# Written orders for the prologue and for the end of the convolution, tap products on four row groups, and late weight splits queued behind other work

## The chip, the cores and the metric

The kernel runs on one core of one Trainium2 chip. The metric is the device time in microseconds (us) of one execution; lower is better. All inputs and the output are fp32.

## The reference

Two layers of a diffusion backbone over 512 tokens of width 1024, with 256 context tokens. Layer 0 mixes with a long convolution (Hyena, 512 channels) beside a neighbourhood attention, layer 1 with a Conformer convolution module; each is followed by a gated feed-forward part of width 2816. Every part is wrapped in two RMS norms with shift, scale and gate from a conditioning vector. What the change touches:

```python
m = jax.nn.silu(cond) @ w_mod + b_mod              # six vectors of 1024: shift, scale, gate, twice
hn = rms_norm(h, g_mix_pre) * (1 + scale1) + shift1
...
# layer 0: the long filters
hdn = jnp.sin(freq[0] * (z @ w1 + b1))             # z: 512 x 33, hidden width 64
hdn = jnp.sin(freq[1] * (hdn @ w2 + b2))
hdn = jnp.sin(freq[2] * (hdn @ w3 + b3))
filt = hdn @ w4                                    # 512 x 1024: forward and backward filter
return filt[:, :512] * decay, filt[:, 512:] * decay
...
# layer 1: the Conformer module
a, g = jnp.split(t @ w_pw1 + b_pw1, 2, axis=-1)
u = a * jax.nn.sigmoid(g)
u = dwconv(u, w_dw, b_dw)                          # 31 taps a channel
u = jax.nn.silu(layer_norm(u, ln_g, ln_b))
return u @ w_pw2 + b_pw2
```

## The kernel before

The tokens lie on the 128 partitions in four chunks, t = 0 to 3. TensorE (PE) does all products. The big ones are three fp32r products each (`mm3`, L278 to L282): the high part of one operand with both parts of the other and its low part with the high one. So every weight block of 512 KB is loaded raw by SP into one of three `raw` buffers and split: ScalarE (ACT) casts the high part (L297), VectorE (DVE) subtracts it for the low part (L298). The class `Stream` issues loads and splits a few blocks ahead of use. The outputs of a split go to working tiles `w`, or to kept tiles `wk` for blocks that are needed again.

A scheduler places all instructions by its own estimate, except on the engines named in a `tc.manual_schedule` block, on which the order of the program text holds. Before, the prologue has such a block for PE alone, in the order of a string of keys ("1 x0 x1 2 x2 x3 3 t0 ... k11"); ACT, DVE, GpSimd (POOL) and SP are placed by the scheduler.

**Prologue.** A small network makes the filters of the long convolution: three layers (PE products at L686, L693 and L716), each followed by a reduction of turns on DVE (L662 to L664, tile `sx`) and a Sin on ACT (L665, tiles `hdn`, then `h`). The two filters (`filt`, keys a and b) are four products each with `w4x` (L743), multiplied with the decay `dec` (L745), split (L746, L747) and negated (L750). `w4x` is first completed by a product on POOL (L710) and two ACT instructions (L717, L718). Meanwhile the four chunks of x get their norm: the sum of squares on ACT (L408), the root on POOL (L401, L403), the scaling on DVE (L498), and are transposed on PE (L705, key t, `pt`) and copied out (L706). The conditioning product (L674, key g, tile `g` from the landed blocks `land`) has eight steps; step k writes to the group of 32 columns k mod 4. The filter spectra (`kspec`, key k, tile `pk`) are mm3 products of the filters with a cosine table, whose high and low part `TFh`, `TFl` come from `tfr` (L727, L728). `columns` (L792) turns the conditioning product to columns, `modulate` applies it, and then the input projection `pz` begins.

**Conformer.** The first pointwise product (`pg`) runs in two halves of 512 channels; `glu` makes `u`. The convolution over time is done as short Fourier transforms: `taps` (L1373) transforms the 31 taps, four products 31 rows deep, each copied to `H` by ACT (L1374); `c_fwd` transforms `u` to `dr` and `di`; `c_prod` (L1404 to L1412) multiplies with `H`, six DVE instructions but for one addition on POOL (L1406), and splits the result to `Yh` and `Yl`; `c_inv` transforms back (`po`), adds the bias (L1426) and takes statistics (L1427); `ln` (L1431 to L1435) norms `yc`; `to_T` transposes it (L515), applies SiLU (ACT, L1438) and splits it into `hTh` (L521) and `hTl` (L522). `gemm_td` is the second pointwise product (`acc`): first all steps k over chunks 0 and 1 for the blocks that are not kept, then per chunk the kept ones, then chunks 2 and 3, whose transposes (`late`) come between. Here no order is written; the scheduler chose it for all engines.

## Time and profile before

| | us |
|---|---|
| median of 3 runs | 1267.14 |
| lowest, highest run | 1264.29, 1267.49 |
| profiled execution | 1264.98 |
| its span in the trace | 1263.2 |

| engine | busy us | share of the span |
|---|---|---|
| PE (TensorE) | 1239.3 | 98% |
| DVE (VectorE) | 815.2 | 65% |
| ACT (ScalarE) | 509.2 | 40% |
| POOL (GpSimd) | 89.4 | 7% |

In rows of the timeline the first number is the start in us from the start of the span, the second the time up to the end of the last instruction of the row; then engine, line, operation, written tile <- read tiles, shapes and count. In brackets stands the idle time of the engine ahead of it and what ended it. A product's own time includes its way through the array, so that products in a row overlap; their pace is read from the starts. An fp32 product leaves two records, an fp32r product or a transpose one. PEld is the loading of weights into the array.

### The profile page before, as it was taken

The page shows a single profiled execution, that of the slowest core. Times are in us where ns is not written, and L with a number is a line of the kernel's source. Part 1 is how long each engine was busy: PE and PEld are TensorE (multiplying, and loading weights), DVE is VectorE, ACT ScalarE, POOL GpSimd, SP SyncE. Part 2 cuts the span into 40 slices and gives each one's busy share as a digit, 9 for nine tenths or more (in the row PEclk, how much of TensorE's full clock was granted, in tenths as well). Part 3 has the DMA queues.
Part 4 walks back from the last instruction along what each step waited for, and adds up shares of the span by engine and source line. Part 5 has one row for each costly group of instructions (what it writes and reads, how often), then busy time and mean ns, then how long its engine had stood idle before and what let it go on. Part 6 is the DMA issues. An engine that isn't in the chain of part 4 may idle for free.

```text
span 1263.2 us, 15493 instructions
## 1 busy us (share of the span) xinstructions
PE 1239.3 (98%) x6044; PEld 1024.2 (81%) x6044; DVE 815.2 (65%) x1072; ACT 509.2 (40%) x788; POOL 89.4 (7%) x157
## 2 busy tenths in 40 slices
PE   6999999999999999999999999999999999999997
PEld 3688888988898888887888887878988888888886
DVE  4577696876567788778534576686687555566233
ACT  5453333576443332336223442233544333344221
POOL 3110000231200000000000100012100000000001
PEclk9999999999999999999999999999999999999999
DMA  9535434743136577764344331120265233332321
GB/s 351 192 114 170 133 110 142 257 152 128 40 101 216 184 240 245 226 193 146 117 132 135 131 104 55 50 101 1 68 203 178 88 98 100 100 100 90 95 84 66
DMA packets 47865, 171.64 MB, mean 136 GB/s; under 512 B 5741, under 2 KB 5772, under 8 KB 47792
## 3 DMA queue, kind: packets, MB, share of 16 engines
q1 hardware_dynamic: 47428, 169.93, 41.4%
q8 instruction: 47, 0.77, 0.2%
q0 software_dynamic: 176, 0.40, 0.1%
q10 hardware_dynamic: 188, 0.33, 0.1%
q14 instruction: 26, 0.21, 0.1%
HBM read 167.76 MB, written 2.10 MB: 134 GB/s over the span
## 4 chain that ended last, share of the span: by engine, by line
PE 76%; DMA 9%; DVE 9%; ACT 2%; issue 2%; POOL 1%; DVEq 0%; POOLq 0%; ACTq 0%
PE pz L280 11%; PE pz L281 11%; PE pz L282 11%; PE acc L282 8%; PE acc L280 8%; PE acc L281 8%; DMA raw<-in_wup 4%; DMA raw<-in_wcol 4%; DVE w L298 3%; PE pg L280 2%; PE pg L282 2%; PE pg L281 2%; DVE acc L430 2%; DMA raw<-in_wgate 1%; ACT w L297 1%
## 5 line engine op out<-in xcount | busy, mean ns | idle before, releaser
L281 PE MATMUL pz<-hTl,w 128*128 128x512 f32 (+1 forms) x920 | 345.4, 376 | 0.0
L280 PE MATMUL pz<-hTh,w 128*128 128x512 f32 (+1 forms) x920 | 344.6, 377 | 0.5 <-DVE hTh L521 0.5
L282 PE MATMUL pz<-hTh,w 128*128 128x512 f32 (+1 forms) x920 | 345.1, 376 | 0.0
L298 DVE TENSOR_TENSOR w<-raw,w 128x1024 fp32r<-128x1024 f32 x159 | 193.9, 1222 | 199.9 <-ACT w L297 194.0
L297 ACT CAST w<-raw 128x1024 fp32r<-128x1024 f32 x159 | 166.4, 1051 | 331.8 <-PE pz L281 132.0
L282 PEld LDWEIGHTS pz<-hTh,w 128*128 128x128 f32 x920 | 173.8, 189 | 31.4
L281 PEld LDWEIGHTS pz<-hTl,w 128*128 128x128 f32 x920 | 173.8, 189 | 30.0 <-DVE hTl L522 0.4
L280 PEld LDWEIGHTS pz<-hTh,w 128*128 128x128 f32 x920 | 173.0, 189 | 31.0 <-DVE hTh L521 1.0
L430 DVE SCALAR_TENSOR_TENSOR acc<-raw,sc,acc 128x1024 f32<-128x1024 f32 x74 | 95.4, 1289 | 41.4 <-DMA raw<-in_wgate 20.8
L281 PE MATMUL acc<-w,gs 128*128 128x512 f32 x256 | 99.6, 389 | 0.0
L282 PE MATMUL acc<-w,gs 128*128 128x512 f32 x256 | 98.4, 390 | 0.5 <-DVE gs L1317 0.5
L280 PE MATMUL acc<-w,gs 128*128 128x512 f32 x256 | 97.0, 389 | 0.0
L879 ACT ACTIVATE cv<-pz,pk 128x512 f32<-128x512 f32 x88 | 67.6, 772 | 0.7 <-PE pz L282 0.7
L881 DVE SCALAR_TENSOR_TENSOR cv<-pz,pk,cv 128x511 f32<-128x511 f32 x88 | 65.6, 747 | 1.8
L880 DVE SCALAR_TENSOR_TENSOR cv<-pz,pk,cv 128x511 f32<-128x511 f32 x88 | 65.1, 744 | 0.2 <-ACT cv L879 0.2
L1279 ACT ACTIVATE cv<-cv 128x512 f32<-128x512 f32 x44 | 27.7, 629 | 81.6 <-DVE cv L881 81.5
L282 PEld LDWEIGHTS acc<-w,gs 128*128 128x128 f32 x256 | 48.0, 188 | 10.9 <-DVE gs L1317 0.9
L280 PEld LDWEIGHTS acc<-w,gs 128*128 128x128 f32 x256 | 48.1, 188 | 10.1 <-DVE cv L881 0.2
L281 PEld LDWEIGHTS acc<-w,gs 128*128 128x128 f32 x256 | 48.1, 188 | 9.9
L298 DVE TENSOR_TENSOR wk<-raw,wk 128x1024 fp32r<-128x1024 f32 x30 | 37.1, 1245 | 29.0 <-ACT wk L297 28.9
L536 DVE TENSOR_TENSOR py<-acc,gg 128x512 f32<-128x512 f32 x32 | 21.8, 688 | 49.1 <-ACT py L408 49.1
L399 POOL TENSOR_SCALAR t<-t,t 128x1 f32<-128x1 f32 x19 | 7.0, 369 | 636.6 <-ACT py L408 628.1
(327 smaller groups left out, 1934.5 us busy)
## 6 DMA issues: line engine op xcount, KB each, us to landing
raw<-in_wup SPq DMA_DIRECT2D x88, 512.0 KB, 3.6
raw<-in_wcol SPq DMA_DIRECT2D x48, 512.0 KB, 4.6
raw<-in_wdn SPq DMA_DIRECT2D x44, 512.0 KB, 3.6
raw<-in_wgate SPq DMA_DIRECT2D x32, 512.0 KB, 4.4
raw<-in_pw SPq DMA_DIRECT2D x24, 512.0 KB, 3.9
raw<-in_win SPq DMA_DIRECT2D x20, 512.0 KB, 3.5
land<-in_wmod SPq DMA_DIRECT2D x16, 512.0 KB, 10.4
BM<-in_rpb SPq DMA_DIRECT2D x8, 512.0 KB, 3.4
```

Of the source, the lines that this page charges most:

```text
L280: PE.matmul(o, ah, bh, start=start, stop=False)
L281: PE.matmul(o, ah, bl, start=False, stop=False)
L282: PE.matmul(o, al, bh, start=False, stop=stop)
L297: A.copy(hi, r)
L298: V.tensor_tensor(lo, r, f(hi), op=ALU.subtract)
L399: G.tensor_scalar(v, sums[0], sums[1], EPS, op0=ALU.add, op1=ALU.add)
L430: V.scalar_tensor_tensor(acc, rs[k], ck_, init if k == 0 else acc, op0=ALU.mult, op1=ALU.add)
L536: V.tensor_tensor(p_[:, sl], y2[i], gg[:, sl], op=ALU.mult)
L879: A.activation(dst, pz, AF.Identity, bias=pc(bk, i), scale=pc(wk + "1", i))
L880: V.scalar_tensor_tensor(dst[:, 1:w], pz[:, 0:w - 1], pc(wk + "0", i), dst[:, 1:w], op0=ALU.mult, op1=ALU.add)
L881: V.scalar_tensor_tensor(dst[:, 0:w - 1], pz[:, 1:w], pc(wk + "2", i), dst[:, 0:w - 1], op0=ALU.mult, op1=ALU.add)
L1279: A.activation(cv[:, 0], cv[:, 0], AF.Silu, bias=0.0, scale=1.0)
```

## The change

The computation stays the same; the change has five parts.

1. **Prologue.** PE, ACT and DVE follow the program order up to the end of filter b, PE alone from there to the end of the prologue. 23 dummy products of a zero tile `warm` (128 by 128, fp32) are put on PE ahead of layer 1 (5), behind it (3), ahead of layer 3 (5) and ahead of filter a (10). The steps are cut finer: sums of squares (`x_sum`) and scalings (`x_scale`) apart, layer 3 and its reduction apart, filters by channel group and step. The two ACT instructions on `w4x` go behind the first and the second Sin. Filter a follows the third Sin, then four of the eight transposes with the table split, then filter b; the other transposes stand between halves of the spectra. The eight steps of the conditioning product become two batches of four. SP loads the decay ahead of the table.
2. **Taps.** The four tap products get operands padded to 32 rows and laid on four groups of 32 partitions, so that each has rows of its own, and are issued together behind the first half's `glu`, into four PSUM tiles.
3. **c_prod.** The addition goes from POOL to DVE, cast and low part are done in halves.
4. **End of the convolution.** From the first pointwise product of chunk 3 to the end of the second pointwise product PE follows the program: the inverse transforms of chunk 1 before the last step of the first pointwise product, those of the first half's chunks 2 and 3 behind it, then the transposes, the last forward transform, and the steps k = 0 to 2 of the second pointwise product before the inverse transforms that need the last `c_prod`.
5. **Late splits.** While `behind` holds an instruction, the scheduler queues the low-part subtractions of new splits behind it: behind the last one of `to_T`, then behind the last one of `c_prod`, until the last inverse transforms are issued.

On ACT, the start of the prologue up to the third Sin. Before (L717, L718: `w4x`; L665: Sin; L408: sums of squares):

```order
L717 ACTIVATE w4x_80<-w4x_80 64x512
L372 CAST onesr<-ones 128x128
L387 COPY SCT_117<-sc 128x8
L392 ACTIVATE SCT_117<-pk 128x8
L718 COPY w4x_80<-w4x_80 64x512
L665 ACTIVATE hdn_180<-sx_190 128x256
L408 ACTIVATE junk_195,t_196<-xc_84 128x1024
L408 ACTIVATE junk_203,t_204<-xc_85 128x1024
L408 ACTIVATE junk_219,t_220<-xc_86 128x1024
L665 ACTIVATE hdn_180<-sx_214 128x256
L408 ACTIVATE junk_227,t_228<-xc_87 128x1024
L665 ACTIVATE h_59_246<-sx_247 128x512
```

After (the same steps at L735, L741, L686 and L426):

```order
L390 CAST onesr<-ones 128x128
L405 COPY SCT_120<-sc 128x8
L410 ACTIVATE SCT_120<-pk 128x8
L686 ACTIVATE hdn_183<-sx_198 128x256
L735 ACTIVATE w4x_83<-w4x_83 64x512
L426 ACTIVATE xn_208,t_209<-xc_87 128x1024
L686 ACTIVATE hdn_183<-sx_218 128x256
L426 ACTIVATE xn_228,t_229<-xc_88 128x1024
L741 COPY w4x_83<-w4x_83 64x512
L426 ACTIVATE xn_255,t_256<-xc_89 128x1024
L426 ACTIVATE xn_262,t_263<-xc_90 128x1024
L686 ACTIVATE h_59_269<-sx_270 128x512
```

Both `w4x` instructions stood ahead of the first Sin; now one stands behind the first and the other behind the second, and the sums are spread 1, 1 and 2 between the Sins.

On PE, the first place of the conditioning product (L674) before, between the last transposes and the filters (L743, all eight in a row):

```order
L674 MATMUL g_311<-land_146,SCT_117 32x512
L674 MATMUL g_313<-land_146,SCT_117 32x512
L674 MATMUL g_315<-land_148,SCT_117 32x512
L674 MATMUL g_317<-land_148,SCT_117 32x512
L743 MATMUL pf_319<-w4x_80,h_59_246 128x512
L743 MATMUL pf_325<-w4x_80,h_59_246 128x512
L743 MATMUL pf_331<-w4x_80,h_59_246 128x512
L743 MATMUL pf_337<-w4x_80,h_59_246 128x512
L743 MATMUL pf_347<-w4x_80,h_59_246 128x512
L743 MATMUL pf_353<-w4x_80,h_59_246 128x512
L743 MATMUL pf_359<-w4x_80,h_59_246 128x512
L743 MATMUL pf_365<-w4x_80,h_59_246 128x512
```

After, the start of its first batch (L695), behind the fourth half of the spectra and long behind both filters:

```order
L695 MATMUL g_460<-land_149,SCT_120 32x512
L695 MATMUL g_460<-land_153,SCT_120 32x512
L695 MATMUL g_460<-land_157,SCT_120 32x512
L695 MATMUL g_460<-land_161,SCT_120 32x512
L695 MATMUL g_465<-land_149,SCT_120 32x512
L695 MATMUL g_465<-land_153,SCT_120 32x512
L695 MATMUL g_465<-land_157,SCT_120 32x512
L695 MATMUL g_465<-land_161,SCT_120 32x512
L695 MATMUL g_470<-land_151,SCT_120 32x512
L695 MATMUL g_470<-land_155,SCT_120 32x512
L695 MATMUL g_470<-land_159,SCT_120 32x512
L695 MATMUL g_470<-land_163,SCT_120 32x512
```

Step 0 ran alone, and steps 1 to 3 came after the filters; now four steps, one for each group of 32 columns, stand next to one another for each output tile `g`.

On DVE, the second half's middle `c_prod` before (L1404 to L1412), where the tiles `wk` are low parts of weights (L298):

```order
L1404 TENSOR_TENSOR cy_6754<-dr_6740,H_6165 128x512
L1408 TENSOR_TENSOR ct_6755<-dr_6740,H_6166 128x512
L298 TENSOR_TENSOR wk_6964<-raw_6925,wk_6963 128x1024
L1405 TENSOR_TENSOR ct_6755<-di_6741,H_6166 128x512
L1407 TENSOR_TENSOR cy_6754<-di_6741,H_6165 128x512
L298 TENSOR_TENSOR wk_6982<-raw_6927,wk_6981 128x1024
L298 TENSOR_TENSOR wk_7000<-raw_6949,wk_6999 128x1024
L1409 TENSOR_TENSOR cy_6754<-cy_6754,ct_6755 128x512
L298 TENSOR_TENSOR wk_7006<-raw_6967,wk_7005 128x1024
L1412 TENSOR_TENSOR Yl_6763<-cy_6754,Yh_6762 128x1024
L1426 TENSOR_TENSOR yc_6791<-po_6790,bd_6167 128x512
```

After, the last `c_prod` (L1516 to L1521) with the splits (L305) around it:

```order
L1516 TENSOR_TENSOR cy_6948<-dr_6934,H_6194 128x512
L1517 TENSOR_TENSOR ct_6949<-di_6935,H_6195 128x512
L1516 TENSOR_TENSOR cy_6948<-di_6935,H_6194 128x512
L1517 TENSOR_TENSOR ct_6949<-dr_6934,H_6195 128x512
L305 TENSOR_TENSOR w_6965<-raw_6524,w_6964 128x1024
L1518 TENSOR_TENSOR cy_6948<-cy_6948,ct_6949 128x512 x2
L1521 TENSOR_TENSOR Yl_6951<-cy_6948,Yh_6950 128x512 x2
L305 TENSOR_TENSOR w_6989<-raw_6530,w_6988 128x1024
L305 TENSOR_TENSOR wk_7007<-raw_6968,wk_7006 128x1024
L305 TENSOR_TENSOR wk_7061<-raw_6970,wk_7060 128x1024
```

Four subtractions stood inside one `c_prod`, between its steps; in the new order one does inside the last `c_prod`, and the next ones stand behind its `Yl`.

The diff, cut to its core:

```diff
+    k31 = np.concatenate([k31, np.zeros((1, 256))], 0)
+    k31 = np.concatenate([k31[:, :128]] * 2 + [k31[:, 128:]] * 2, 0)
...
+    wd = np.concatenate([g["cf_w_dw"][0], np.zeros_like(g["cf_w_dw"][0][:1])], 0)
+    a["wdw"] = np.concatenate([wd[:, :512], wd[:, 512:]] * 2, 0)
...
-        V.tensor_tensor(lo, r, f(hi), op=ALU.subtract)
+        with ExitStack() as queued:
+            if behind:
+                queued.enter_context(tc.issue_after(behind[0]))
+            V.tensor_tensor(lo, r, f(hi), op=ALU.subtract)
         return hi, lo
...
+    warm = cpool.tile([P, P], F32, name="warm")
+    V.memset(warm, 0.0)
+    warm_ps = pspool.tile([P, 512], F32, name="warm_ps", tag="ps")
+
+    def warm_up(n):
+        for _ in range(n):
+            PE.matmul(warm_ps[:, 0:P], warm, warm, start=True, stop=True)
 
...
-            V.tensor_tensor(hT[1][kp][:, :, sl], X, f(o_h), op=ALU.subtract)
+            done = V.tensor_tensor(hT[1][kp][:, :, sl], X, f(o_h), op=ALU.subtract)
+        return done
...
+            if k in between:
+                between[k]()
...
-    for key in "x0 x1 x2 x3 t0 t1 d0 d1 l0 l1 l2 l3 l4 l5 l6 l7 l8 l9 l10 l11 l12 l13 l14 l15".split():
+    for key in "x0 x1 x2 x3 d0 d1 t0 t1 l0 l1 l2 l3 l4 l5 l6 l7 l8 l9 l10 l11 l12 l13 l14 l15".split():
...
-    def x_norm(c):
-        xns[c] = norm_chunk(xc[c])
+    def x_sum(c):
+        xns[c] = s4(F32, (P, 1024), "xn")
+        xns[c, "r"] = rstd([sumsq(xc[c], xns[c])])
+
+    def x_scale(c):
+        V.tensor_scalar(xns[c], xc[c], xns[c, "r"], None, op0=ALU.mult)
...
+    def w4_neg():
+        A.mul(w4x[0:64, 512:1024], w4x[0:64, 0:512], -1.0)
+
+    def w4_decay():
         G.tensor_tensor(w4x[64:128, 0:512], w4x[64:128, 0:512], zt[64:128, 512:1024], op=ALU.mult)
-        pm = [ps("pf") for _ in range(2)]
...
+    def w4_copy():
         A.copy(w4x[64:128, 512:1024], w4x[64:128, 0:512])
...
-        for i in range(2):
-            hv = flat(TFh[i], "p a b -> p (a b)")
-            with tc.issue_after(sin3.ins):
-                A.copy(hv, tfr[i])
-            V.tensor_tensor(flat(TFl[i], "p a b -> p (a b)"), tfr[i], f(hv), op=ALU.subtract)
...
+    early = ExitStack()
+    early.enter_context(tc.manual_schedule(engines={mybir.EngineType.PE, mybir.EngineType.Activation,
+                                                    mybir.EngineType.DVE}))
+    warm_up(5)
+    layer1()
+    warm_up(3)
+    w4_decay()
+    w4_neg()
+    x_sum(0)
+    layer2()
+    warm_up(5)
+    x_sum(1)
+    x_scale(0)
+    layer3(0)
+    warm_up(10)
+    w4_copy()
+    x_sum(2)
+    x_sum(3)
+    layer3(1)
+    for ch in range(4):
+        filt("a", ch, "p")
+    x_scale(1)
+    x_scale(2)
+    filt("a", 0, "m")
+    filt("a", 1, "m")
+    x_scale(3)
+    filt("a", 0, "l")
+    for ch in (2, 3):
+        filt("a", ch, "m")
+        filt("a", ch - 1, "l")
+    filt("a", 3, "l")
+    for i in range(2):
+        x_T(i)
+        table_hi(i)
+        table_lo(i)
+    for i in range(2, 4):
+        x_T(i)
+    for ch in range(4):
+        filt("b", ch, "p")
+        filt("b", ch, "m")
+        if ch:
+            filt("b", ch - 1, "l")
+    filt("b", 3, "l")
+    early.close()
     order_pe = ExitStack()
     order_pe.enter_context(tc.manual_schedule(engines={mybir.EngineType.PE}))
-    for key in "1 x0 x1 2 x2 x3 3 t0 t1 t2 t3 t4 t5 t6 t7 g0 a b g123 k00 k01 g4567 k100 c m k101 k11".split():
-        steps[key[0]](*(int(i) for i in key[1:]))
+    kspec(0, 0, 0)
+    x_T(4)
+    x_T(5)
+    for lo in range(2):
+        negate("a", lo)
+    kspec(1, 0, 0)
+    x_T(6)
+    x_T(7)
+    for lo in range(2):
+        negate("b", lo)
+    kspec(0, 0, 1)
+    kspec(1, 0, 1)
+    gemv_k(0, 1, 2, 3)
+    gemv_k(4, 5, 6, 7)
+    kspec(0, 1, 0)
+    columns()
+    modulate()
+    kspec(0, 1, 1)
+    kspec(1, 1)
     order_pe.close()
     hT = hTs[0]
 
@@ -1359,19 +1463,23 @@
...
-    SP.dma_start(kk[:31, 0:256], a["k31"])
+    SP.dma_start(kk[:, 0:128], a["k31"])
     wd = s4(F32, (P, 1024), "wd")
-    SP.dma_start(wd[:31], a["wdw"])
+    SP.dma_start(wd[:, 0:512], a["wdw"])
...
-    def taps(cs, hf):
-        pm = ps("pm")
-        PE.matmul(pm, kk[:31, cs * P:(cs + 1) * P], wd[:31, hf * 512:(hf + 1) * 512], start=True, stop=True)
-        A.copy(H[cs][:, hf * 512:(hf + 1) * 512], pm)
+
+    def taps():
+        pms = [ps("pm") for _ in range(4)]
+        for i, pm in enumerate(pms):
+            rs = slice(32 * i, 32 * i + 32)
+            PE.matmul(pm, kk[rs, 0:P], wd[rs, 0:512], start=True, stop=True)
+        for i in (0, 2, 1, 3):
+            A.copy(H[i // 2][:, i % 2 * 512:(i % 2 + 1) * 512], pms[i])
...
-        V.tensor_tensor(y[:, 0], pr_, H[0][:, hs], op=ALU.mult)
-        V.tensor_tensor(tm[:, 0], pi_, H[1][:, hs], op=ALU.mult)
-        G.tensor_tensor(y[:, 0], y[:, 0], tm[:, 0], op=ALU.add)
-        V.tensor_tensor(y[:, 1], pi_, H[0][:, hs], op=ALU.mult)
-        V.tensor_tensor(tm[:, 1], pr_, H[1][:, hs], op=ALU.mult)
-        V.tensor_tensor(y[:, 1], y[:, 1], tm[:, 1], op=ALU.subtract)
         yh_, yl_ = s4(F32R, n="Yh"), s4(F32R, n="Yl")
-        A.copy(yh_, y)
-        V.tensor_tensor(yl_, y, f(yh_), op=ALU.subtract)
+        for i, (p0, p1, op) in enumerate(((pr_, pi_, ALU.add), (pi_, pr_, ALU.subtract))):
+            V.tensor_tensor(y[:, i], p0, H[0][:, hs], op=ALU.mult)
+            V.tensor_tensor(tm[:, i], p1, H[1][:, hs], op=ALU.mult)
+            V.tensor_tensor(y[:, i], y[:, i], tm[:, i], op=op)
+            A.copy(yh_[:, i], y[:, i])
+        for i in range(2):
+            done = V.tensor_tensor(yl_[:, i], y[:, i], f(yh_[:, i]), op=ALU.subtract)
+        prod_end[:] = [done.ins]
         return yh_, yl_
 
     parts = {0: [(0, 0)], 1: [(0, 1), (1, 2)], 2: [(1, 1), (2, 2)], 3: [(2, 3)]}
...
-    taps(0, 0)
+    taps()
...
-        if k < 3:
-            taps(1 - k % 2, (k + 1) // 2)
...
+    last = ExitStack()
+    last.enter_context(tc.manual_schedule(engines={mybir.EngineType.PE}))
     pw1_t(3, range(4), True, False)
     Y1.append(c_prod(1, *c_fwd(1, U1)))
-    pw1_t(3, range(4, 8), False, False)
-    c_inv(0, 2, Y0)
+    pw1_t(3, range(4, 7), False, False)
     c_inv(1, 1, Y1)
     ln(1)
-    U1.append(glu(1, 3))
+    pw1_t(3, range(7, 8), False, True)
     mark("ln+pw2")
-    fw = c_fwd(2, U1)
+    c_inv(0, 2, Y0)
+    c_inv(0, 3, Y0)
     lT = alloc_hT()
-    to_T([yc[0], yc[1]], 0, lT, silu_ev)
-    Y1.append(c_prod(1, *fw))
-    c_inv(0, 3, Y0)
+    behind.append(to_T([yc[0], yc[1]], 0, lT, silu_ev).ins)
+    Y1.append(c_prod(1, *c_fwd(2, U1)))
     dmp("cd", yc[0])
     b2 = s4(F32, (P, 1024), "b2")
     SP.dma_start(b2, a["bpw2"].rearrange("a b -> (a b)").partition_broadcast(P))
...
+    def third():
+        behind[:] = prod_end
+
+    def fourth():
         for t in (2, 3):
             c_inv(1, t, Y1)
+        for t in (2, 3):
             ln(t)
+        behind.clear()
+
+    def late1():
         to_T([yc[2], yc[3]], 1, lT, silu_ev)
 
     after, late2, st2 = stage_end(1, 1, 1, 2, pre=add_b2)
     gemm_td(8, 4, lambda k: (hk(lT, k, 0), hk(lT, k, 1)), after, 4,
-            late=late1)
+            late=late1, between={0: third, 2: fourth})
+    last.close()
     hT = st2["hT"]
     dmp("h3", h[0])
```

More of the change, by code (lines that the diff above doesn't have):

```diff
@@ L541, in post_chunk, with gemm_td @@
             V.scalar_tensor_tensor(hc[:, sl], p_[:, sl], r, hc[:, sl], op0=ALU.mult, op1=ALU.add)
-    def gemm_td(nk, keep, act, after, nxt, late=None, nbg=2):
+    def gemm_td(nk, keep, act, after, nxt, late=None, nbg=2, between={}):
         acc = [[None, None] for _ in range(4)]
@@ new lines, in layer3 @@
+    def layer3(part):
+        if part == 0:
+            pm = [ps("pf") for _ in range(2)]
+            h3s.append(pm)
+            for i, o, src, ro in ((0, slice(0, 256), slice(0, 256), 0), (1, slice(256, 512), slice(0, 256), 0),
+                                  (0, slice(0, 255), slice(1, 256), 64), (0, slice(255, 256), slice(255, 256), 64),
+                                  (1, slice(255, 511), slice(0, 256), 64), (1, slice(511, 512), slice(255, 256), 64)):
+                rs = slice(64 * i, 64 * i + 64)
+                PE.matmul(pm[i][ro:ro + 64, o], fl[rs, 128:192], h2[rs, src], start=True, stop=True)
+            return
+        pm = h3s.pop()
@@ L719, in layer3, with table_hi @@
         h3s.append(s4(F32, (P, 1024), "h3"))
-        sin3 = sin_stage([(pm[0], slice(None), slice(0, 256)), (pm[1], slice(None), slice(256, 512)),
-                          (pm[1], slice(64, 128), slice(255, 256))], 2, h3s[0][:, 0:512], 512)
+        sin_stage([(pm[0], slice(None), slice(0, 256)), (pm[1], slice(None), slice(256, 512)),
+                   (pm[1], slice(64, 128), slice(255, 256))], 2, h3s[0][:, 0:512], 512)
         G.memset(h3s[0][64:128, 511:512], 0.0)
-        for i in range(2):
-            hv = flat(TFh[i], "p a b -> p (a b)")
-            with tc.issue_after(sin3.ins):
-                A.copy(hv, tfr[i])
-            V.tensor_tensor(flat(TFl[i], "p a b -> p (a b)"), tfr[i], f(hv), op=ALU.subtract)
+    def table_hi(i):
+        A.copy(flat(TFh[i], "p a b -> p (a b)"), tfr[i])
@@ L730, in tfs, with table_lo @@
+    def table_lo(i):
+        V.tensor_tensor(flat(TFl[i], "p a b -> p (a b)"), tfr[i], f(flat(TFh[i], "p a b -> p (a b)")), op=ALU.subtract)
     def tfs(lo, ch, cs, fc):
```

40 lines of the change are left out of this document (18 added, 22 removed).

## The prediction, made before the changed kernel was run

> **What bounds the kernel now.** I read the profiled execution from the top: the page's busy line, then the busy time in windows of 40 us, then the timeline in the three places that the diff touches. The page's first line gives the engines.
>
> ```profile
> PE 1239.3 (98%) x6044; PEld 1024.2 (81%) x6044; DVE 815.2 (65%) x1072; ACT 509.2 (40%) x788; POOL 89.4 (7%) x157
> ```
>
> TensorE (PE) is busy 98% of the span of 1263.2 us, so only two things can help: less time in which PE waits, and the same PE work in less time. The windows show where it waits. Columns: length, then busy time and count of PE, PEld, DVE, ACT and POOL, granted clock, DMA share, GB/s.
>
> ```profile
> 0.00:40.00 40.00, 27.99 (x117) 15.04 (x118) 20.28 (x34) 23.53 (x42) 10.24 (x31) 1.00 0.90 336
> ...
> 320.00:360.00 40.00, 39.74 (x255) 35.80 (x254) 20.06 (x31) 15.57 (x38) 7.09 (x15) 1.00 0.01 3
> 800.00:840.00 40.00, 37.82 (x168) 29.70 (x167) 29.77 (x38) 13.88 (x17) 4.47 (x6) 1.00 0.32 105
> ```
>
> A middle stretch (320) leaves 0.26 us idle; the first 40 us leave 12.0, the stretch at 800 leaves 2.2. The change works in these two and in the taps at 757, where PE is busy with small products. The prologue is a chain of small steps; here are its links, first PE.
>
> ```profile
> 9.14 1.12 PE L693 MATMUL pf<-hdn,fl 64*64 64x256 f32 x4 [5.05 <-ACT hdn L665]
> 13.16 1.25 PE L716 MATMUL pf<-hdn,fl 64*64 64x256 f32 x12 [2.91 <-ACT hdn L665]
> ...
> 16.59 5.46 PE L705 MATMUL pt<-ident,junk 128*128 128x128 f32 x29 [1.04 <-DVE junk L498]
> 21.98 3.62 PE L674 MATMUL g<-land,SCT 128*32 128x512 f32 x8
> 25.53 7.14 PE L743 MATMUL pf<-w4x,h 128*128 128x512 f32 x16
> 32.60 3.63 PE L674 MATMUL g<-land,SCT 128*32 128x512 f32 x24
> ...
> 47.27 3.64 PE L674 MATMUL g<-land,SCT 128*32 128x512 f32 x32
> ...
> 63.64 0.42 PE L280 MATMUL pz<-hTh,w 128*128 128x512 f32 x1
> ```
>
> PE waits 5.05 and 2.91 us for the first two Sins (hdn) and is then without a break from 16.59 to `pz`, the input projection, at 63.64. So the prologue costs its start at 16.59 plus 47.05 us of dense work. The three L674 rows are the conditioning product, 8, 24 and 32 records in practically the same 3.6 us: products on different groups of 32 columns run at once, so a pass costs the same however many groups it fills. ACT and DVE explain the start.
>
> ```profile
> 5.99 0.63 ACT L717 ACTIVATE w4x<-w4x 64x512 f32<-64x512 f32 x1 [0.61 <-DMA w4x<-in_fw]
> ...
> 8.03 0.61 ACT L718 COPY w4x<-w4x 64x512 f32<-64x512 f32 x1 [1.01 <-POOL w4x L710]
> 8.67 0.42 ACT L665 ACTIVATE hdn<-sx 128x256 f32<-128x256 f32 x1
> 8.99 1.04 ACT L408 ACTIVATE junk<-xc 128x1024 f32<-128x1024 f32 x1
> ...
> 12.69 0.42 ACT L665 ACTIVATE hdn<-sx 128x256 f32<-128x256 f32 x1 [0.38 <-DVE sx L664]
> ...
> 18.98 0.63 ACT L665 ACTIVATE h<-sx 128x512 f32<-128x512 f32 x1 [4.83 <-DVE sx L664]
> 19.52 1.03 ACT L727 CAST TFh<-tfr 128x1024 fp32r<-128x1024 f32 x1
> ```
>
> ```profile
> 5.23 0.54 DVE L662 TENSOR_SCALAR sx<-pf,pk,turn 128x256 f32<-128x256 f32 x1
> ...
> 6.14 0.43 DVE L664 SCALAR_TENSOR_TENSOR sx<-sx 128x256 f32<-128x256 f32 x1
> ...
> 16.45 1.31 DVE L662 TENSOR_SCALAR sx<-pf,pk,turn 128x256 f32<-128x256 f32 x3
> ```
>
> The first Sin's input is ready at 6.14 + 0.43 = 6.57, but ACT starts it at 8.67: the copy L718, which waits for POOL, stands ahead of it. The third layer's product ends at 13.16 + 1.25 = 14.41, and DVE takes it up only at 16.45.
>
> **Prologue, the start.** With the two w4x steps behind the Sin, it starts at about 6.6, 2.05 earlier, and L693 at 9.14 - 2.05 = 7.1. That ends at 8.2; a turn reduction with nothing between takes 6.57 - 5.23 = 1.34 us, so sx is ready at 9.6. ACT then still has the 1.04 us of a sum of squares in hand: Sin 2 at about 9.9. The next product starts 13.16 - 12.69 = 0.47 after it, at 10.4, and ends at 11.6. The third reduction took 18.98 - 16.45 = 2.53: 14.1. By then ACT has done, from 10.3, the other three sums (3 x 1.04) and L718 (0.61), which end at 14.1 too, so Sin 3 runs from 14.2 to 14.8 and filter a's product starts at 14.9. The dense start moves from 16.59 to 14.9: **1.7 us**. SP now loads the decay's two blocks ahead of the table's two: at the 336 GB/s of the first window 512 KB take 1.6 us, so the table comes 3.1 later and the decay 3.1 earlier. The table's cast at 19.52 had not waited for a load; the spectra that read it now begin at about 23.8, behind filter a (3.57), sixteen transposes (1.8) and filter b (3.57), with casts and subtractions of about 1 us each ahead of them. That fits closely; I count it at nothing, with 1 us for a late table inside the bounds.
>
> **Prologue, the dense work.** The conditioning product's eight steps run in two passes of four instead of passes of one, three and four, which is **3.6 us** less. The third part is PE's pace. The granted clock says 1.00 throughout, but these windows of the transposes do not:
>
> ```profile
> 19.00:19.50 0.50, 0.50 (x4) 0.50 (x4) 0.00 (x0) 0.00 (x0) 1.00 1.04 426
> ...
> 21.00:21.50 0.50, 0.50 (x7) 0.50 (x6) 0.00 (x0) 0.50 (x3) 1.00 1.05 426
> ```
>
> ```profile
> L792 PE MATMUL pm<-ident,R x16: 271/273/273, 53.7 to 55.3; 128*128 128x128 f32 x16
> ```
>
> Four or five transposes in half a microsecond until 21.0, seven after: PE starts slow and doubles about 4.4 us after 16.59, where it became dense. The 29 transposes took 21.98 - 16.59 = 5.39; at the pace of the sixteen of L792 (15 steps in 1.6 us, 0.11 each) all 32 need 3.6, of which three lay ahead of 16.59 before. That is 1.8 less if the 23 dummy products have PE at speed by 14.9; I take **1.5**, since four stretches of transposes now alternate with other products. The dummies cost nothing if they end before the product behind them is ready. A 512-column product of L743 takes 7.14 / 8 = 0.89, a 128-column one a quarter, 0.22, or 0.45 at half pace. The ten ahead of filter a take 2.2 to 4.5 us from 11.6, so 13.8 to 16.1 against 14.9: between 0 and 1.2 late. Sum: 6.8, `pz` at 56.8. Bounds: 2.0, with all ten slow (1.2) and filter a's first half (3.57) at half pace as well; and 7.1.
>
> In a sentence apart: the Trainium skill ("TensorE: Matmul & The Clock Gate", Part 1) has half rate until a busy window of about 3.4 us is over, the window running free, so that the count of slow products differs from run to run; the change of pace at 21.0 agrees roughly, and by that rule the 1.2 could appear in some runs and not in others.
>
> **Taps.** Each of the four products stood alone between groups of pointwise products.
>
> ```profile
> 757.19 1.12 PE L1373 MATMUL pm<-wd,k 31*128 31x512 f32 x2
> 758.24 0.50 PE L280 MATMUL pg<-w,hTh 128*128 128x512 f32 x1
> ```
>
> ```profile
> L1373 PE MATMUL pm<-wd,k x8: 587/640/692, 757.2 to 772.4; 31*128 31x512 f32 x8
> ```
>
> One costs 758.24 - 757.19 = 1.05, four (8 records) 4.2. L716 above is the nearest row for products on separate groups of rows: six products, four of them 256 columns wide, took 1.25, hardly more than the two of L693 (1.12). Side by side the four should take about one product's 1.05 plus some: 1.3, a gain of **2.9**. Bounds: 0, if they queue, to 3.15.
>
> Apart: the Trainium skill ("TensorE: Matmul & The Clock Gate", Part 3) gives 3.07 times for four products of 32 rows and 512 columns, by which the four would take 1.4 and the gain be 2.8; no run here shows that shape yet.
>
> **The end of the convolution.** PE before:
>
> ```profile
> 828.83 0.39 PE L280 MATMUL dr<-u,FT 128*128 128x512 f32 x1
> ...
> 830.19 0.38 PE L515 MATMUL pt<-ident,yc 128*128 128x128 f32 x2
> ...
> 831.81 0.50 PE L281 MATMUL po<-Yl,FT 128*128 128x512 f32 x1 [0.76 <-DVE Yl L1412]
> ...
> 836.06 0.50 PE L280 MATMUL dr<-u,FT 128*128 128x512 f32 x1 [0.80 <-ACT u L1383]
> ...
> 838.38 1.53 PE L515 MATMUL pt<-ident,yc 128*128 128x128 f32 x12 [0.39 <-DVE yc L1435]
> 840.50 0.50 PE L280 MATMUL acc<-w,hTh 128*128 128x512 f32 x1 [0.59 <-DVE hTh L521]
> ...
> 866.48 2.00 PE L515 MATMUL pt<-ident,yc 128*128 128x128 f32 x16
> 869.13 0.50 PE L280 MATMUL acc<-w,hTh 128*128 128x512 f32 x1 [0.65 <-DVE hTh L521]
> ```
>
> Six products from 828.83 to 830.19 give 0.227 each. From 828.83 to 840.50, 11.67 us, there are 24 of these (5.4) and 16 transposes (1.8): 4.4 us are lost to waits and to switching between the two. Add 0.6 at 869.13: 5.0. In the new order each wait has cover: behind the inverse transforms of t = 1 the last pointwise product, behind it those of t = 2 and 3 of the first half (24 products, 5.4 us, in which the layer norm of t = 1 and `u` end), and the product of the last forward transform waits behind the steps k = 0 to 2 of the second pointwise product (3 x 12 x 0.227 = 8.2 us, against some 5 us that c_prod takes). Walking the written order with these durations, the second token half (869.13) starts at 864.1. I take **4.9**. If cover fails, the wait comes back, at most the 5.0; the price of late weights is a rival.
>
> DVE gets three more half-width instructions a c_prod, six times, for an add of 0.68 that POOL did:
>
> ```profile
> 828.68 0.68 DVE L1409 TENSOR_TENSOR cy<-cy,ct 128x512 f32<-128x512 f32 x1
> ```
>
> DVE is busy 29.8 of the 40 us there, so this costs nothing by itself. The late subtractions are queued behind the transposes' last instruction and c_prod's last: what is behind them is the release of the three raw buffers, and so the next weight loads.
>
> **Sum.** 6.8 + 2.9 + 4.9 = 14.6. The profiled execution took 1264.98 (1.8 beside its span), so 1250.4 against it. It stands 2.2 below the median of the runs, 1267.14, from which the forecast is **1252.5**. 0.3% is 3.8 us, about what a measurement can tell from no change.
>
> **Rivals.** Late weights. A split held back holds its raw buffer, and the next load cannot start.
>
> ```profile
> 825.68 3.07 DVE L298 TENSOR_TENSOR wk<-raw,wk 128x1024 fp32r<-128x1024 f32 x2
> ```
>
> ```profile
> L297 ACT CAST w<-raw 128x1024 fp32r<-128x1024 f32 x159 | 166.4, 1051 | 331.8 <-PE pz L281 132.0
> ...
> raw<-in_pw SPq DMA_DIRECT2D x24, 512.0 KB, 3.9
> ```
>
> A round is 3.9 for the load, 1.05 for the cast and about 1.2 for the subtraction: 6.2 us. Before, DVE did the splits between the steps of c_prod (3.07 for two), long ahead of use. By my walk the last two are ready within 0.5 us of their use, so this is the weak point. One round that PE waits for gives 1252.5 + 6.2 = 1258.7 (chance 0.11); two give 1264.9, no change (0.04). Three rounds in a row give 1271.1, **slower**; it decides from 14.6 / 6.2 = 2.4 rounds, and the order leaves PE nothing else to do meanwhile. Against it: three buffers let loads overlap (0.03).
>
> Slow PE: the dummies end late, with filter a at half pace: 1252.5 + 4.8 = 1257.3, or 1253.7 with the 1.2 alone. For: the pace rose only after 4.4 us of dense work, and gaps remain between the dummies; against: 2.2 to 4.5 us of them stand right ahead of filter a (0.11).
>
> Taps queue: 1252.5 + 2.9 = 1255.4. L716 speaks against it (0.06).
>
> The prologue's end is set by something else, the loads (336 GB/s over the first 40 us) or the modulation ahead of `pz`, so that `pz` stays at 63.64: 1252.5 + 6.8 = 1259.3. Against: before, PE had no wait from 17 to 63.64 (0.05).
>
> **Numbers.** The forecast has 0.60, the rivals the rest. All ends of gain together (7.1 + 3.15 + 5.0 = 15.3) from the fastest run, 1264.29, give 1249.0; the high end is one late round, 1258.7. Outside lie two and three rounds and the last rival (0.12) and a little of the others. Faster: all but two and three rounds, 0.93; same 0.04; slower 0.03.
>
> **What would show it.** Right: the first Sin at 6.6, filter a at 14.9, `pz` near 56.8; four overlapping tap products in 1.1 to 1.4 us; from `dr` of the last transform on no wait over 0.3 us, and the second token half 4.9 us earlier relative to the taps' end. Wrong: PE waits for a `w` or `wk` subtraction in the second pointwise product; filter a beyond 16.1; tap products starting 0.9 apart.

## The result and the profile after

| | before | after |
|---|---|---|
| median, us | 1265.72 (6 runs, 1262.99 to 1270.05) | 1252.36 (6 runs, 1250.60 to 1254.67) |
| profiled execution, us | 1264.98 | 1254.67 |
| its span, us | 1263.2 | 1252.9 |

The ratio is 0.9895, 95% interval 0.9874 to 0.9917: 13.3 us less, between 10.5 and 15.9. The forecast was 1252.5. Timed again on another chip beside its predecessor (e12 below) the changed kernel took 1249.34 against 1264.49.

The page's first line and the windows, which stood at 27.99 and 37.82 us of PE in 40 before:

```profile
PE 1238.9 (99%) x6090; PEld 1028.7 (82%) x6090; DVE 815.9 (65%) x1085; ACT 509.2 (41%) x794; POOL 81.2 (6%) x151
```

```profile
0.00:40.00 40.00, 37.41 (x194) 26.05 (x198) 23.41 (x39) 25.86 (x46) 10.50 (x31) 1.00 0.90 336
800.00:840.00 40.00, 40.00 (x185) 33.01 (x185) 33.36 (x52) 14.43 (x22) 1.89 (x4) 1.00 0.18 56
```

The prologue on PE, with the dummies as `warm_ps`, then the taps and three places of the second pointwise product: a late weight, the start of the second token half, and a low part that comes late:

```profile
7.11 1.12 PE L714 MATMUL pf<-hdn,fl 64*64 64x256 f32 x4 [0.94 <-ACT hdn L686]
8.16 2.50 PE L364 MATMUL warm_ps<-warm 128*128 128x128 f32 x10
10.59 1.25 PE L752 MATMUL pf<-hdn,fl 64*64 64x256 f32 x12
11.77 2.75 PE L364 MATMUL warm_ps<-warm 128*128 128x128 f32 x20
15.12 3.68 PE L783 MATMUL pf<-w4x,h 128*128 128x512 f32 x8 [0.61 <-POOL t L421]
18.64 1.91 PE L730 MATMUL pt<-ident,xn 128*128 128x128 f32 x16
...
36.80 7.07 PE L695 MATMUL g<-land,SCT 128*32 128x512 f32 x64
...
56.59 0.42 PE L284 MATMUL pz<-hTh,w 128*128 128x512 f32 x1
...
753.28 1.14 PE L1480 MATMUL pm<-wd,k 32*128 32x512 f32 x8
...
847.02 0.50 PE L285 MATMUL acc<-wk,hTh 128*128 128x512 f32 x1 [0.76 <-DVE wk L305]
...
857.77 0.50 PE L284 MATMUL acc<-w,hTh 128*128 128x512 f32 x1
...
858.71 0.51 PE L286 MATMUL acc<-w,hTl 128*128 128x512 f32 x1 [0.20 <-DVE hTl L540]
```

The first and the third Sin on ACT, ahead of layer 2 and of filter a:

```profile
6.64 0.42 ACT L686 ACTIVATE hdn<-sx 128x256 f32<-128x256 f32 x1 [0.81 <-DVE sx L685]
14.39 0.63 ACT L686 ACTIVATE h<-sx 128x512 f32<-128x512 f32 x1 [0.28 <-DVE sx L685]
```

Layer 2 starts at 7.11 instead of 9.14 and filter a at 15.12. The bracket at filter a names POOL, whose step on `t` ended at 15.06, but this product reads `w4x` and `h`: what it waits for is the third Sin, which ends at 15.02. The sixteen transposes take 1.91 us, 0.12 each, where the first ones took 0.21. The conditioning product is one stretch of 7.07 us instead of three of 3.6, and `pz` starts 7.05 us earlier. The four tap products are one row.

To see where the time goes, the span is cut at starts of products. The columns are: start of `pz`; from the first score product of the attention (`sc`) to the first product of the first feed-forward part's second half (`acc<-w,gs`), where nothing was changed; from the first tap to the last second pointwise product (`acc<-wk,hTh`). Of the rest, the stretch from `pz` to `sc` (161.4), the two up to the taps and the end after `acc` each differ by under 1 us between all these profiles.

| profile of | `pz` | `sc` to `gs` | taps to `acc` | median, us (ratio, interval) |
|---|---|---|---|---|
| before | 63.6 | 364.4 | 135.3 | |
| after | 56.6 | 367.6 | 128.5 | 1252.36 (0.9895, 0.9874 to 0.9917) |
| e12, after again | 56.4 | 363.7 | 127.6 | 1249.34 (0.9883, 0.9867 to 0.9898) |
| e1, prologue alone | 56.2 | 367.3 | 135.0 | 1259.02 (0.9957, 0.9941 to 0.9972) |
| e2, taps alone | 63.9 | 367.8 | 131.0 | 1260.77 (0.9974, 0.9966 to 0.9983) |
| e3, parts 3 to 5 alone | 64.0 | 363.3 | 133.5 | 1263.77 (0.9994, 0.9983 to 1.0005) |
| e4, no dummies | 58.7 | 364.1 | 130.0 | 1254.92 (0.9929, 0.9915 to 0.9943) |
| e5, no queue | 57.1 | 365.1 | 130.1 | 1255.98 (0.9936, 0.9924 to 0.9948) |
| e6, queue for the first place | 56.4 | 365.2 | 133.0 | 1257.24 (0.9951, 0.9938 to 0.9963) |
| e7, three batches | 58.0 | 367.1 | 127.3 | 1254.65 (0.9927, 0.9915 to 0.9939) |
| e8, taps on the same rows | 56.4 | 366.0 | 133.0 | 1254.14 (0.9921, 0.9906 to 0.9937) |
| e9, ten dummies | 56.8 | 368.7 | 127.2 | 1253.75 (0.9912, 0.9898 to 0.9926) |
| e10, addition on POOL | 56.5 | 367.0 | 127.3 | 1251.46 (0.9897, 0.9881 to 0.9912) |
| e11, four raw buffers | 62.1 | 363.8 | 131.3 | 1257.83 (0.9942, 0.9928 to 0.9955) |

In the pair of profiles, prologue (7.05) and taps to `acc` (6.7) bring 13.8 us; 3.2 of them are lost again in the unchanged middle and 0.3 at the end, so that the spans differ by 10.3. The middle runs in the same order on every engine in all these profiles but e11's, and still takes 363.3 to 368.7 us. A median carries part of this swing too, so what a part is worth is read from the stretches where it is under about 3 us.

### The profile page after: what moved, and what is told of

It reads as the page before. It is cut to its first block, busy times and chain, and to the rows that moved or that the text cites. A ratio compares the mean times of both kernels' runs of the same rounds, so it can differ in the third digit from the quotient of the medians.

```text
span 1252.9 us, 15592 instructions
## 1 busy us (share of the span) xinstructions
PE 1238.9 (99%) x6090; PEld 1028.7 (82%) x6090; DVE 815.9 (65%) x1085; ACT 509.2 (41%) x794; POOL 81.2 (6%) x151
## 4 chain that ended last, share of the span: by engine, by line
PE 70%; DMA 12%; DVE 11%; ACT 3%; issue 3%; POOL 0%; SPq 0%; DVEq 0%; POOLq 0%; ACTq 0%
PE pz L284 10%; PE pz L285 10%; PE pz L286 10%; PE acc L286 8%; PE acc L285 8%; PE acc L284 8%; DMA raw<-in_wup 4%; DVE w L305 4%; DMA raw<-in_wcol 3%; DMA raw<-in_wgate 3%; PE pg L284 2%; PE pg L286 2%; PE pg L285 2%; ACT w L301 2%; DVE acc L448 2%
## 5 line engine op out<-in xcount | busy, mean ns | idle before, releaser
L305 DVE TENSOR_TENSOR w<-raw,w 128x1024 fp32r<-128x1024 f32 x159 | 193.9, 1222 | 200.3 <-ACT w L301 199.9
L305 DVE TENSOR_TENSOR wk<-raw,wk 128x1024 fp32r<-128x1024 f32 x30 | 36.4, 1221 | 32.4 <-ACT wk L301 32.2
L301 ACT CAST wk<-raw 128x1024 fp32r<-128x1024 f32 x30 | 31.3, 1050 | 46.7 <-DMA raw<-in_wdn 27.3
## 6 DMA issues: line engine op xcount, KB each, us to landing
land<-in_wmod SPq DMA_DIRECT2D x16, 512.0 KB, 10.9
```

Of the source, the lines that this page charges most:

```text
L301: A.copy(hi, r)
L305: V.tensor_tensor(lo, r, f(hi), op=ALU.subtract)
```

## The experiments

Theory A: the gains of the parts add up, and what the middle loses is chance. Rival B: the attention, reached 7 us earlier, gives part of it back. On the end of the convolution, theory L: what waits remain come from weights that are late because the queued splits hold the raw buffers. Ratios are against the kernel before, timed beside each group on the same chip (medians 1264.38 for e1 to e4, 1263.21 for e5 to e8, 1264.49 for e9 to e12).

**e1, the prologue alone.**

The kernel before, with this part of the change (cut to its start and end):

```diff
-    for key in "1 x0 x1 2 x2 x3 3 t0 ...
+    warm_up(5)
+    layer1()
...
+    kspec(1, 1)
```

> The kernel before with the new prologue alone (parts 2 to 5 of the change left out). Theory A, the parts add up: the input projection starts at about 56.6 instead of 63.64 and the 7 us arrive at the end, so about 6.8 us less than the kernel before. Rival B, the attention gives part of it back: in the changed kernel the first to the last score product took 62.4 us (218.0 to 280.4) against 60.1 before (225.0 to 285.1), and the next feed-forward part lost another 1; by this the same 62.4 shows here and only about 4 us arrive.

```profile
56.20 0.42 PE L280 MATMUL pz<-hTh,w 128*128 128x512 f32 x1
```

`pz` comes 7.4 us earlier, and 5.4 us arrive in the median (3.5 to 7.5 by the interval). The middle took 367.3, 2.9 more than before. That looks like rival B until e2.

**e2, the taps alone.**

The kernel before, with this part of the change (and the padded operands, not shown):

```diff
-    taps(0, 0)
+    taps()
-        if k < 3:
-            taps(1 - k % 2, (k + 1) // 2)
```

> The kernel before with the four tap products side by side alone. Theory A: one stretch of about 1.1 us instead of four of 1.05, and 3.1 us less at the end. Rival: the H copies come late or PSUM runs out of tiles, so that the first forward transform or pointwise product waits, and 1 us or less arrives. With the prologue as before the attention should take its 60.1 us under both theories on the attention.

```profile
759.74 0.39 PE L286 MATMUL pg<-wk,hTl 128*128 128x512 f32 x1
760.06 1.14 PE L1380 MATMUL pm<-wd,k 32*128 32x512 f32 x8
761.13 0.50 PE L284 MATMUL pg<-w,hTh 128*128 128x512 f32 x1
```

All four take 1.07 us from start to the next product, as much as one before. 3.6 us less in the median (2.1 to 4.3). And the middle took 367.8, though up to the taps every engine's order is that of the kernel before, which took 364.4. The attention took 63.3 of it, not the 60.1 expected; PE waited 1.01 us there, up to 245.5, and the granted clock then read 0.50 from 245.8 to 249.2. So the swing needs no earlier arrival: rival B is not needed to explain e1, though a small effect of that kind is not excluded.

**e3, the end of the convolution alone.** The kernel before, with the new c_prod, `behind`, `between` and

```diff
+    last.enter_context(tc.manual_schedule(engines={mybir.EngineType.PE}))
...
+    last.close()
```

> The kernel before with the new c_prod, the written order at the end of the convolution and the queued late splits, parts 3 to 5, alone. Theory A: no wait between the last forward transform and the second pointwise product, one late weight of under 1 us as in the changed kernel, so 4 to 4.5 us less. Rival: late weights take back more than they did beside the other parts, 2 us or less arrive. The attention should take its 60.1 us.

Nothing that can be measured, between 2.1 us less and 0.6 more: the rival's figure. The profile shows 1.8 us less from the taps to `acc`, and two waits (PE), the second behind a queue on DVE:

```profile
852.75 0.50 PE L281 MATMUL acc<-wk,hTh 128*128 128x512 f32 x1 [0.53 <-DVE wk L301]
...
865.14 0.50 PE L280 MATMUL acc<-w,hTh 128*128 128x512 f32 x1 [1.69 <-DVE hTh L526]
```

```profile
846.27 0.68 DVE L1436 TENSOR_TENSOR yc<-po,bd 128x512 f32<-128x512 f32 x1
849.14 1.22 DVE L301 TENSOR_TENSOR wk<-raw,wk 128x1024 fp32r<-128x1024 f32 x1 [2.18 <-ACT wk L297]
850.29 0.68 DVE L1437 BATCH_NORM_STATS2 st<-yc 128x6 f32<-128x512 f32 x1
```

DVE waits 2.18 us for the cast of a late weight, and the statistics of the layer norm stand behind it in its queue. The delay travels on. Chunk 0's sum of squares on ACT comes late with it, and only behind that stands the SiLU that `hTh` needs:

```profile
862.92 3.74 ACT L1448 ACTIVATE X<-pt,pk 128x256 f32<-128x256 f32 x8
```

It starts 5.2 us after the last transpose (857.70), in the changed kernel 3.6 after it (855.55 and 851.99); the difference is about the wait of 1.69. In the changed kernel both halves' bias and statistics stand ahead of that split. Same source text, other order: DVE is placed by the scheduler's own estimate, and another prologue shifts it, as e4 shows, which differs from the changed kernel in the prologue's dummies alone and has e3's order.

**e4, no dummies.**

```diff
-        for _ in range(n):
+        for _ in range(0):
```

> The changed kernel without the 23 dummy products. Theory: filter a starts at 15.1 as with them, but PE runs its first 4.4 dense microseconds at half pace, which costs half of it: the input projection starts about 2.2 us later (58.8) and the kernel takes 2 us more than with them, 11 less than before. Rival: the three small layers already bring PE to speed, or the dummies only fill idle time, and nothing changes (the projection at 56.6, 13 less than before).

```profile
14.99 6.12 PE L783 MATMUL pf<-w4x,h 128*128 128x512 f32 x8 [3.41 <-POOL t L421]
```

Filter a starts at the same time and takes 6.12 instead of 3.68; `pz` is at 58.7, 2.1 later, as expected. The median loses more than that, 9.5 us gained and not 13.3, and part of it has another place: this kernel got e3's order on DVE and its wait of 1.69, and took 130.0 from the taps to `acc`. e9 is the cleaner test.

**e5, nothing queued.**

```diff
-            if behind:
+            if False:
```

> The changed kernel with the late splits queued behind nothing. Theory L, late weights: the queue holds the raw buffers, loads are issued late, and the waits that remain at the convolution's end (1.0 at a kept weight, up to 1.9 at the first product of chunk 2) come from that; without the queue both go, while c_prod is held up by splits again but hidden behind 8 us of the second pointwise product: from the taps to the end of the second pointwise product 127 us against 128.5 in the changed kernel, 1 us less in all. Rival: the queue is what makes the written order work, and without it PE waits for Yl or hTh as before, 130 us or more, 2 us more in all.

```profile
815.73 0.49 PE L284 MATMUL po<-Yh,FT 128*128 128x512 f32 x1 [1.29 <-ACT Yh L1519]
817.56 0.50 PE L285 MATMUL po<-Yl,FT 128*128 128x512 f32 x1 [1.34 <-DVE Yl L1521]
```

```profile
813.35 1.29 DVE L1518 TENSOR_TENSOR cy<-cy,ct 128x512 f32<-128x512 f32 x2
814.55 2.35 DVE L305 TENSOR_TENSOR wk<-raw,wk 128x1024 fp32r<-128x1024 f32 x2
816.83 1.29 DVE L1521 TENSOR_TENSOR Yl<-cy,Yh 128x512 fp32r<-128x512 f32 x2
```

The waits for weights are gone, as theory L has it, but two splits stand in front of `Yl` and the first inverse transform of the new order waits 2.63 us. I had looked only at the last c_prod; the one before has no cover. The rival holds: 130.1, some 2.7 more than the usual 127.4.

**e6, queued behind the transposes only.**

```diff
-        behind[:] = prod_end
+        behind.clear()
```

> The changed kernel with splits queued behind the transposes' last instruction only, and no longer behind the last c_prod. Theory L: the last kept weights are split in time, so the wait of about 1 us for a kept weight goes and chunk 2 begins without a wait: 127 us from the taps to the end of the second pointwise product, about 1.2 us less than the changed kernel. Rival: the last c_prod comes late and the inverse transforms wait for it, 129 us or more.

```profile
835.04 0.58 PE L285 MATMUL acc<-w,hTh 128*128 128x512 f32 x1 [3.18 <-DVE w L305]
835.41 0.63 PE L286 MATMUL acc<-w,hTl 128*128 128x512 f32 x1
835.84 0.63 PE L284 MATMUL acc<-w,hTh 128*128 128x512 f32 x1
```

```profile
829.16 1.23 DVE L305 TENSOR_TENSOR wk<-raw,wk 128x1024 fp32r<-128x1024 f32 x1 [0.75 <-ACT wk L301]
...
831.37 0.68 DVE L1516 TENSOR_TENSOR cy<-dr,H 128x512 f32<-128x512 f32 x1
...
833.17 0.68 DVE L1517 TENSOR_TENSOR ct<-dr,H 128x512 f32<-128x512 f32 x1
833.77 2.35 DVE L305 TENSOR_TENSOR w<-raw,w 128x1024 fp32r<-128x1024 f32 x2
```

```profile
836.00:837.00 1.00, 1.00 (x4) 0.81 (x3) 1.00 (x3) 0.19 (x1) 0.00 (x0) 0.50 0.62 184
```

The 133.0 is in the rival's range, but neither mechanism is right: the kept weights are in time, but the scheduler has put their splits first, and a weight that is needed at once is split behind four steps of c_prod. After the wait PE's granted clock is 0.50, and a product takes 0.43 instead of 0.227. What counts is what stands ahead in the queue, not how long it is.

**e7, three batches again.**

```diff
-    gemv_k(0, 1, 2, 3)
+    gemv_k(0)
+    gemv_k(1, 2, 3)
```

> The changed kernel with the conditioning product in three batches (one, three and four steps) again, one behind the other at the same place. Theory: one more pass of 3.6 us on PE with nothing to hide it, the input projection at 60.2 instead of 56.6, 3.6 us more in all. Rival: products in different column groups are not the reason for the equal time of the passes and the eight steps cost the same in any batches, no change.

```profile
36.47 8.81 PE L695 MATMUL g<-land,SCT 128*32 128x512 f32 x64
```

8.81 against 7.07 us: 1.7 more, not 3.6. Batches that stand next to each other overlap at their border: step 0's first four records stand alone (36.47 to 37.78), and from its fifth on (38.21) one record of each of steps 1 to 3 starts beside it, 0.43 us from start to start. So of 3.8 us saved (10.9 in three places before) 2.1 come from standing together and 1.7 from one batch less. The taps to `acc` took 127.3 here, with the order of the changed kernel and without its wait for `wk`. The median lies further from the changed kernel's, 0.9927 against 0.9895, with intervals that overlap; `pz` is only 1.4 to 1.6 us later.

**e8, taps together on the same rows.**

```diff
-            rs = slice(32 * i, 32 * i + 32)
-            PE.matmul(pm, kk[rs, 0:P], wd[rs, 0:512], start=True, stop=True)
+            rs, cs, hf = slice(0, 32), i // 2, i % 2
+            PE.matmul(pm, kk[rs, cs * P:(cs + 1) * P], wd[rs, hf * 512:(hf + 1) * 512], start=True, stop=True)
```

> The changed kernel with the four tap products issued together, but all on the first 32 rows. Theory: what counts is that they lie on separate rows; on the same rows they queue for 0.9 us each, 3.6 us instead of 1.1, so about 2.5 us more than the changed kernel. Rival: what counts is that they stand together, since each stop between other products cost 0.2 to 0.3 us; then the products themselves still take 0.9 each and only about 1 us of the 3.4 was from standing together; under the extreme form of it the stretch takes 1.1 here too and nothing changes.

```profile
750.66 4.20 PE L1480 MATMUL pm<-wd,k 32*128 32x512 f32 x8
754.80 0.79 PE L284 MATMUL pg<-w,hTh 128*128 128x512 f32 x1
```

```profile
754.00:756.00 2.00, 2.00 (x5) 1.01 (x4) 1.49 (x2) 0.64 (x2) 0.00 (x0) 0.50 0.78 264
```

4.14 us to the next product instead of 1.07. About 0.5 of that is the clock: the granted clock falls to 0.50 at 753.7, within the last product. The first three products took 2.68 us (750.66 to 753.34), 0.89 each, so that four take 3.6 at full pace, as expected: of the 4.2 before, standing together is worth 0.6 and the separate rows 2.5. From the taps to `acc` it is 4.4 more than in the first profile after, not the 2.5 expected, since the clock stays at 0.50 up to 760.5, 6.8 us in all. One of its five runs took 1375.36, which nothing here explains; the median is not moved by it.

**e9, ten dummies only.**

```diff
-    warm_up(5)
     layer1()
-    warm_up(3)
...
     layer2()
-    warm_up(5)
```

> The changed kernel with only the ten dummy products ahead of filter a; the 13 around the first two layers are left out. All other engines keep their order at the convolution's end, unlike in the kernel without any dummies. Theory: the ten alone, at half pace, take 4.5 us and end 1.2 us after the third Sin, but bring PE to speed for filter a: input projection 57 to 58, at most 1.2 us more than with all 23, where the kernel without any had 58.7. Rival: PE needs more than these; filter a runs at half pace and the projection is at 59 or later, 2 us more.

```profile
11.48 4.12 PE L364 MATMUL warm_ps<-warm 128*128 128x128 f32 x20
15.44 3.60 PE L783 MATMUL pf<-w4x,h 128*128 128x512 f32 x8
```

The ten take 4.0 us up to filter a, where they took 2.75 in the first profile and 2.91 in e12; they hold filter a up by 0.3 to 0.5, and `pz` is at 56.8. By that the other 13 are worth 0.2 to 0.4 us. The median says more, 4.4 above e12's timed beside it, with intervals that barely touch. In the profile the middle took about 5 us more than e12's, in the same order. One place is a weight that came late:

```profile
521.66 0.50 PE L284 MATMUL pz<-hTh,w 128*128 128x512 f32 x1 [1.87 <-ACT w L301]
```

The granted clock then read 0.50 from 523.5 to 526.9. Why the other runs of e9 are as slow is not shown.

**e10, the addition on POOL.**

```diff
-            V.tensor_tensor(y[:, i], y[:, i], tm[:, i], op=op)
+            (V if i else G).tensor_tensor(y[:, i], y[:, i], tm[:, i], op=op)
```

> The changed kernel with the addition in c_prod back on POOL (part 3 undone in its main point). Theory: c_prod is hidden behind the second pointwise product and other products, so neither its 0.6 us on DVE nor the way through POOL shows: 127 to 129 us from the taps to the end of the second pointwise product, the kernel within 1 us of the changed one. Rival: DVE has no slack there, the way over POOL delays Yl, PE waits for it and 1.5 us or more are lost.

127.3 from the taps to `acc`, as in the changed kernel (127.6 in e12), so nothing is lost at that place. The median is 2.1 us above e12's, with intervals that overlap (0.9881 to 0.9912 and 0.9867 to 0.9898); the middle took 367.0 against 363.7 in the two profiles. A difference below 2 us is not settled.

**e11, four raw buffers.**

```diff
-    rpool = ctx.enter_context(tc.tile_pool(name="raw", bufs=3))
-    spool = ctx.enter_context(tc.tile_pool(name="s", bufs=31))
+    rpool = ctx.enter_context(tc.tile_pool(name="raw", bufs=4))
+    spool = ctx.enter_context(tc.tile_pool(name="s", bufs=30))
```

> The changed kernel with four raw buffers instead of three, at the price of one of 31 buffers of the general pool; the scheduler may move other instructions too. Theory L: the wait for a kept weight at the convolution's end (0.8 in the changed kernel's profile, none in another execution of the same order) comes from loads that wait for a buffer; with a fourth it goes: no wait for wk there, 127.3 us or less from the taps to the end of the second pointwise product. Rival: the loads are late for another reason, SP's order or the queue itself, and a wait of 0.8 or more for w or wk stays.

There is no wait for `w` or `wk` in the second pointwise product, as theory L expects. But the fourth buffer costs more elsewhere (`pz` at 62.1). It lets SP issue the input projection's first weight at 30.5 instead of 42.2, and the scheduler puts its cast on ACT ahead of the copies of the last transposes. The cast waits 9.23 us for the load, PE waits for the copies in the middle of the conditioning product, and the granted clock reads 0.50 from 42.5 to 45.9:

```profile
40.72 1.04 ACT L301 CAST w<-raw 128x1024 fp32r<-128x1024 f32 x1 [9.23 <-DMA raw<-in_win]
41.67 1.07 ACT L731 COPY xT<-pt 128x512 f32<-128x512 f32 x2
```

```profile
42.30 6.20 PE L695 MATMUL g<-land,SCT 128*32 128x512 f32 x40 [3.86 <-ACT xT L731]
```

And the last but one forward transform waits twice:

```profile
811.78 0.49 PE L284 MATMUL dr<-u,FT 128*128 128x512 f32 x1 [1.08 <-ACT u L1491]
813.04 0.50 PE L285 MATMUL dr<-u,FT 128*128 128x512 f32 x1 [0.77 <-DVE u L1492]
```

So the 131.3, where 127.3 was expected, says nothing against the theory, and nothing for it beyond the missing wait, since the order around it changed too.

**e12, the changed kernel again,** without an edit.

> The changed kernel itself, on the chip of the three others, so that they can be compared. Theory: the stretch from the first score product of the attention to the second feed-forward part's start varies by up to 4 us from execution to execution without any change of order (364.1 to 367.8 so far), and the stretch at the convolution's end by about 1 us with the weights' landing; this profile differs from the first one of the same kernel by that, and the median is 12 us below the kernel before. Rival: both stretches repeat within 0.5 us for the same kernel.

363.7 in the middle against 367.6 in the first profile of the same kernel on another chip. Two of the places, from the first profile; this one has no wait there. They make 0.9 of the 3.9:

```profile
516.36 0.50 PE L286 MATMUL pz<-hTh,w 128*128 128x512 f32 x1 [0.42 <-DVE w L305]
...
523.00 0.50 PE L286 MATMUL pz<-hTh,w 128*128 128x512 f32 x1 [0.52 <-DVE w L305]
```

At the end of the convolution (taps, kept weight, second token half) the kept weight is in time but for 0.23 us (842.06 - 841.60 - 0.227):

```profile
749.24 1.14 PE L1480 MATMUL pm<-wd,k 32*128 32x512 f32 x8
...
841.60 0.39 PE L284 MATMUL acc<-wk,hTh 128*128 128x512 f32 x1
842.06 0.50 PE L285 MATMUL acc<-wk,hTh 128*128 128x512 f32 x1
...
852.80 0.50 PE L284 MATMUL acc<-w,hTh 128*128 128x512 f32 x1
```

What moves the landing of weights from one execution to the next stays open; no experiment here controls it.

## Why the prediction was right, point by point

- **The sum.** 14.6 was forecast; 13.3 (10.5 to 15.9) and, on another chip, 15.1 were measured. That the median lies 0.1 us from the forecast of 1252.5 is luck: it was counted from a median of 1267.14, and more runs put that at 1265.72. The parts alone give 5.4, 3.6 and 0.6, 9.6 in all. Some of what is missing is the end of the convolution, which gains only 1.8 in e3's profile, with another order on DVE; the rest can lie within the intervals.
- **Start of the prologue.** Right: the first Sin at 6.64 (6.6 forecast), layer 2 at 7.11 (7.1), the third Sin at 14.39 (14.2), filter a at 15.12 (14.9).
- **Dense work.** Right: 3.8 for the conditioning product (3.6), and PE at speed for filter a. The rival "slow PE" did not come: without the 13 early dummies it costs 0.4 at `pz`, not 1.2 (e9), and without all of them 2.1 (e4). The 3.57 that the prediction counts for filter a's first half is the whole of filter a; in e4 the row is 2.4 longer.
- **Taps.** Right in kind, too small: 2.9 forecast. The four cost 4 x 1.05, and the product behind each 0.1 more than usual: 4.6 together, against 1.07 + 0.1 now, so 3.4 gained. The step that failed is "about one product's 1.05 plus some: 1.3": four cost what one did. (e2's stretch to `acc` is 4.2 shorter; the waits at the convolution's end happen to be smaller in it too, 0.59 for `Yl` and not 0.76.)
- **End of the convolution.** Right up to the start of the second token half where the weights are in time, too large behind it: 4.9 forecast. From the taps to that start it took 111.9 us before (757.19 to 869.13), 104.5 in the first profile (753.28 to 857.77) and 103.6 in e12 (749.24 to 852.80). Less the taps' 3.4, this is 4.0 and 5.0 gained; most of the difference is the kept weight that came 0.76 late in the first profile, where the prediction had its last two weights ready within 0.5 of their use. From that start to the last `acc` the new order takes 0.7 more (24.0 against 23.3), of which some is the waits for `hTl` behind it. So 3.3 and 4.2 are left at the last `acc`. The step that failed is the 4.9 that goes into the sum: it ends the walk at the start of the second half, takes the last wait of 0.6 as gone, and has no wait on the way. It also left out the DVE queue, in which a late weight delays the layer norm (1.69 in e3 and e4).
- **DVE's extra work** is hidden at that place (e10). **Late weights** was the right rival to fear, at 0.8 to 2.5 us (first profile, e4) instead of a round of 6.2.
- So the taps were taken 0.5 and the prologue 0.3 to 0.6 too small, the end of the convolution 0.7 to 1.6 too large. The total is closer than its terms because these errors partly cancel, which is luck as well.

## What to carry to other kernels

Where one engine is busy nearly all the time, sum its idle gaps at the place of the change and ask of each wait what the new order puts in front of it; then do the same for the queue of the engine that releases it, since a split or copy that waits for a transfer holds up everything behind it. A scheduler's order on the other engines can shift when an unrelated part changes, so that a part tried alone need not show what it gives in the whole. Compare unchanged stretches of two profiles before the difference is explained: here the same program, on two chips, swung by 3.9 us in one.
